# Two of four units of the recurrence's output product, moved behind the last head's output in the program

## The chip, the core and the metric

One core of one Trainium2 chip runs the whole program once. The metric is the device time of one execution in microseconds (us), here the median of three runs of the kernel before. Five engines work beside each other, each through its own queue of instructions and strictly in that queue's order: TensorE (PE in the profile, with its weight loads as PEld), VectorE (DVE), ScalarE (ACT), GpSimd (POOL), and SyncE (SP), which issues the loads from HBM. They wait for each other by semaphores.

## What is computed

Two model blocks follow each other on a sequence of 512 tokens of width 1024. The change touches the first half of the second block only. There a normed input is projected to two mixers: a matrix memory (four heads of width 128, run forward and backward, with the context's 256 tokens in front) and a gated recurrence (four heads of width 128). Both outputs are normed, gated and projected back into the residual stream. Cut to that:

```python
pl = _modulate(_rmsnorm(xl, norm1_w[l]), sh1, sc1) @ w_in[l]
pc = _modulate(_rmsnorm(xc, norm1_w[l]), sh1c, sc1c) @ w_in[l]
ml_l, ml_c = _mlstm_mixer(pl[..., :ML_COLS], pc[..., :ML_COLS], ...)   # norm(h) * sigmoid(o)
hg_l, hg_c = _hgrn_mixer(pl[..., ML_COLS:], pc[..., ML_COLS:], ...)    # norm(o) * silu(g)
xl = xl + g1 * (jnp.concatenate([ml_l, hg_l], axis=-1) @ w_out[l])
```

The rows of `w_out` that belong to the recurrence need only `hg_l`, which is ready before the matrix memory starts. So this part of the product (`wout2h` in the kernel) may be done anywhere in the matrix memory's stretch.

## The kernel before, in words

Everything is kept with the model's width on the 128 partitions and the 512 tokens along the free dimension. Every fp32 product is made of three passes over operands split in a high and a low part: `mm3` records matmuls at L211, L212 and L213, each 128x512. A weight unit of 128x1024 comes by `wload`: a load of 512 KB (tile `raw`, two buffers, L225), a copy of the high part on ScalarE (`wh`, three buffers, L189) and the low part on VectorE or GpSimd (`wl`, three buffers, L192). `wload` runs at a raised priority, so that it stands some places ahead of where it was called.

The program is written head by head, and a scheduler then sets each engine's queue: it follows the written order as priority, but takes an instruction earlier or later where its own timing model says that the operands come so. Tiles of one tag rotate over a fixed number of buffers: 4 PSUM banks for `mm`, 3 for `aux`, 1 for `sm`. A tile that comes round to a bank waits until the former tile in it has been read.

`mlstm` (L1773) runs the matrix memory. Per head `h`:
- `pj(h)` projects keys and queries and convolves them (`caccm`, nine taps: on VectorE mostly, a few by ScalarE as `ctapm` and GpSimd), and `silu` makes `mk` and `mq` of them on ScalarE. This runs one head ahead.
- `ml_weights` (L1919) makes the decay weights `mW`, one per direction: a row broadcast by a matmul (L1916, tile `ps_sm`, tag `sm`), an add on VectorE, four exponentials on ScalarE. For heads 2 and 3 it is called at the end of heads 0 and 1.
- `ml_within` (L1931) transposes the keys (L1939, `mkT`), makes the scores (L1944), and multiplies them into `mW` on VectorE.
- `ml_states` (L1950) makes the chunk states of each direction: five matmuls (L1970, `ps_aux`), chained decays on VectorE and ScalarE (`mC`), and a row broadcast (L1916) that scales the queries (`mqw`).
- `ml_out` (L1986) makes the outputs, four groups of four matmuls (L1994, L1995); each group takes one of the three `aux` banks, and VectorE and ScalarE read it out (`mdn`, `myt`, `yml`).

In the last turn of the loop, where no next head is to be projected, two other pieces stand ahead of the last head's states: `hgout((0, 1, 2))`, three of the four units of the recurrence's output product (24 matmuls per unit: two output tiles of four `mm3`, reading `mhH` and `mhL`; each tile is added to the residual `x` by VectorE in `res`), and `proj_tok` of `w2o`, the gate's projection (four weight units, 96 matmuls, which read `wh` with `h3H`). `proj_tok` accumulates all four units into four `mm` tiles at once and hands them over in `pso`. Behind the loop their sigmoids follow on ScalarE (`og`), then the fourth unit, `hgout((3,))`. The calls of `bact` between two `batch()` calls are ordered on ScalarE as a group, so that its function tables are swapped seldom: the four `og` stand behind the silu of head 3, which stands behind the exponentials of head 3's weights. After that come the head norms (transposes at L1617, `moH`, `moL`) and the matrix memory's part of the output product (`wout2m`).

Quoted, since the order matters:

```python
            for h in range(4):
                self.ahead = 400
                if h < 3:
                    nxt = silu(*pj(h + 1))
                else:
                    pso = []
                    hgout((0, 1, 2))
                    self.proj_tok(I["w2o"], lambda b, ps: pso.append(ps), False)
                self.ahead = 150
                Cq = self.ml_states(pw, h, kT, kq[1])
```

Of the kernel before, what the change touches and what calls it, by code (L numbers as in the profile page):

```python
# [179 lines left out]
class Kern:  # L180
# [1592 lines left out]
    def mlstm(self, st, hs, cs):  # L1773
# [25 lines left out]
        def pj(h):  # L1799
            pl, pc = self.proj2(I["w2k"][h], hs, cs)  # L1800
            raw = p.tile([128, T], F32, name="mraw", tag="mraw", bufs=2)
            self.act(raw, pl)
            rc = p.tile([128, TC], F32, name="mrawc", tag="mrawc", bufs=1)
            self.act(rc, pc)
            k = self.conv(raw, self.cwm[:, 4 + h], p, 8, 64, 3, "m")
            kc = self.conv(rc, self.cwm[:, 4 + h], p, 1, 256, 0, "mc")
            pl, _ = self.proj2(I["w2q"][h], hs, None)
            raw = p.tile([128, T], F32, name="mraw", tag="mraw", bufs=2)
            self.act(raw, pl)
            q = self.conv(raw, self.cwm[:, h], p, 8, 64, 3, "m")  # L1810
            return k, kc, q

        def silu(k, kc, q):
            kf = p.tile([128, NT], F32, name="mk", tag="mk", bufs=2)
            self.bact(kf[:, 0:TC], kc, AF.Silu)
            self.bact(kf[:, TC:], k, AF.Silu)
            qf = p.tile([128, T], F32, name="mq", tag="mq", bufs=2)
            self.bact(qf, q, AF.Silu)
            return kf, qf
# [9 lines left out]
        def res(m, ps, sl):  # L1829
            self.stt(self.x[m][:, sl], ps, g1[:, m:m + 1], self.x[m][:, sl], mul, add)  # L1830

        def hgout(us):

            for u in us:
                W = self.wload(I["wout2h"][u])
                for i in range(2):
                    ps = self.mmtile()
                    for k in range(4):
                        c = slice(512 * i + 128 * k, 512 * i + 128 * k + 128)
                        self.mm3(ps, (W[0][:, c], W[1][:, c]), (self.mHL[0][:, k], self.mHL[1][:, k]), k == 0, k == 3)  # L1840
                    res(2 * u + i, ps, slice(0, T))

        with ExitStack() as st1:
            pw = self.pool(st1, "mlw")
            self.batch()
            W = [self.ml_weights(pw, i) for i in range(2)]
            self.batch()
            kq = silu(*kq)
            kT = self.ml_within(pw, 0, *kq, W[0])
# [3 lines that stand above are left out]
                    nxt = silu(*pj(h + 1))  # L1853
                else:
                    pso = []
                    hgout((0, 1, 2))
                    self.proj_tok(I["w2o"], lambda b, ps: pso.append(ps), False)
                self.ahead = 150
                Cq = self.ml_states(pw, h, kT, kq[1])
                if h < 3:  # L1860
                    kq = nxt
                    kT = self.ml_within(pw, h + 1, *kq, W[h + 1])
                self.ml_out(pw, h, W[h], *Cq, yml)
                if h < 2:
                    self.batch()
                    W.append(self.ml_weights(pw, h + 2, "sm"))
                    self.batch()
            self.batch()
            for b in range(4):
                o = p.tile([128, 512], F32, name="og", tag=("mraw", "caccm")[b % 2], bufs=2)  # L1870
                self.bact(o, pso[b], AF.Sigmoid)
                self.tt(o, o, self.mlw, mul, nc.gpsimd)
                og.append(o)
            hgout((3,))

            self.stc.close()
            pm = self.pool(st, "mlm", side="right")
            mo = [pm.tile([128, 4, T], F32R, name="mo" + n) for n in "HL"]
            for h in range(4):
                self.head_norm(p, yml, h, og, mo)  # L1880
            self.dump("yml", yml)
# [240 lines left out]
```

## Time and profile before

| what | us |
|---|---|
| median of 3 runs (1603.66 to 1607.11) | 1603.7 |
| the profiled execution, its own time | 1606.45 |
| its span, first to last instruction | 1604.7 |
| TensorE busy in the span | 1551.7 (97%) |
| VectorE busy | 1107.8 (69%) |
| ScalarE busy | 764.3 (48%) |
| GpSimd busy | 385.0 (24%) |

The span is what the trace shows; the execution's own time has 1.75 us more around it. Busy time of TensorE counts matmuls whose ends are modelled and overlap, so its waits are better read from the starts of its matmuls, in order of time. In the rows that stand further down, a line of the timeline has the start, the time taken, engine, source line, operation, output and inputs, and in brackets how long the engine sat idle before it and what released it.

### The profile page before, as it was taken

The page shows a single profiled execution, that of the slowest core. Times are in us where ns is not written, and L with a number is a line of the kernel's source. Part 1 is how long each engine was busy: PE and PEld are TensorE (multiplying, and loading weights), DVE is VectorE, ACT ScalarE, POOL GpSimd, SP SyncE. Part 2 cuts the span into 40 slices and gives each one's busy share as a digit, 9 for nine tenths or more (in the row PEclk, how much of TensorE's full clock was granted, in tenths as well). Part 3 has the DMA queues.
Part 4 walks back from the last instruction along what each step waited for, and adds up shares of the span by engine and source line. Part 5 has one row for each costly group of instructions (what it writes and reads, how often), then busy time and mean ns, then how long its engine had stood idle before and what let it go on. Part 6 is the DMA issues. An engine that isn't in the chain of part 4 may idle for free.

```text
span 1604.7 us, 22771 instructions
## 1 busy us (share of the span) xinstructions
PE 1551.7 (97%) x8577; PEld 1296.0 (81%) x8577; DVE 1107.8 (69%) x2055; ACT 764.3 (48%) x1405; POOL 385.0 (24%) x327
## 2 busy tenths in 40 slices
PE   7999997999999999999999999999989999999997
PEld 6778786677888888888888888878879888888886
DVE  8887546676679754863436777478877798676745
ACT  5453536563444213452346777646654664343322
POOL 1110124113000000000020001314320897556552
PEclk9999999999999999999999999999999999999998
DMA  5222411004356764833222111111211322232322
GB/s 192 82 74 67 133 56 47 14 21 133 103 199 214 245 197 130 258 111 103 82 65 71 33 51 54 47 56 64 66 59 66 102 95 92 98 100 92 96 86 82
DMA packets 58733, 157.84 MB, mean 98 GB/s; under 512 B 11904, under 2 KB 18816, under 8 KB 58496
## 3 DMA queue, kind: packets, MB, share of 16 engines
q1 hardware_dynamic: 58624, 156.40, 30.4%
q8 instruction: 67, 1.10, 0.3%
q14 instruction: 42, 0.34, 0.1%
HBM read 152.57 MB, written 2.10 MB: 96 GB/s over the span
## 4 chain that ended last, share of the span: by engine, by line
PE 81%; DVE 11%; ACT 5%; issue 2%; POOL 1%; DMA 1%; SPq 0%; DVEq 0%; ACTq 0%
PE ps_mm L211 23%; PE ps_mm L213 22%; PE ps_mm L212 22%; PE ps_sm L1129 2%; DVE wl L192 2%; DVE caccm L201 2%; PE ps_mm L1118 1%; PE ps_aux L1574 1%; ACT L189 1%; ACT wh L189 1%; PE ps_sm L787 1%; DVE caccf L201 1%; PE ps_aux L1563 1%; PE ps_aux L1096 1%; PE ps_sm L1590 0%
## 5 line engine op out<-in xcount | busy, mean ns | idle before, releaser
L189 ACT ACTIVATE wh<-raw 128x1024 fp32r<-128x1024 f32 (+3 forms) x234 | 236.8, 1013 | 498.7 <-PE ps_mm L212 361.6
L192 DVE TENSOR_TENSOR wl<-raw,wh 128x1024 fp32r<-128x1024 f32 (+2 forms) x162 | 196.7, 1215 | 99.3 <-ACT wh L189 93.5
L201 DVE SCALAR_TENSOR_TENSOR caccf<-ps_mm,cwf,caccf 128x441 f32<-128x441 f32 (+2 forms) x278 | 188.5, 695 | 30.9 <-ACT ctapf L189 24.8
L192 POOL TENSOR_TENSOR wl<-raw,wh 128x1024 fp32r<-128x1024 f32 (+2 forms) x72 | 160.7, 2233 | 158.7 <-ACT wh L189 158.6
L213 PE MATMUL ps_mm<-h4H,wl 128*128 128x512 f32 (+1 forms) x352 | 131.2, 375 | 0.0
L212 PE MATMUL ps_mm<-h4L,wh 128*128 128x512 f32 (+1 forms) x352 | 131.1, 375 | 0.0
L211 PE MATMUL ps_mm<-h4H,wh 128*128 128x512 f32 (+1 forms) x352 | 129.7, 377 | 0.6 <-DVE caccf L201 0.4
L192 POOL TENSOR_TENSOR rr<-rv,nhalf 128x2 f32<-128x2 f32 x9 | 8.5, 946 | 431.3 <-DVE rv L198 431.3
L211 PE MATMUL ps_mm<-h2H,wh 128*128 128x512 f32 (+1 forms) x280 | 103.8, 372 | 0.0
L213 PE MATMUL ps_mm<-h2H,wl 128*128 128x512 f32 (+1 forms) x280 | 103.6, 371 | 0.0
L212 PE MATMUL ps_mm<-h2L,wh 128*128 128x512 f32 (+1 forms) x280 | 103.6, 371 | 0.0
L211 PE MATMUL ps_mm<-aH,wh 128*128 128x512 f32 (+1 forms) x272 | 102.6, 377 | 0.5 <-DVE x L192 0.5
L213 PE MATMUL ps_mm<-aH,wl 128*128 128x512 f32 (+1 forms) x272 | 102.7, 378 | 0.0
L212 PE MATMUL ps_mm<-aL,wh 128*128 128x512 f32 (+1 forms) x272 | 102.4, 377 | 0.0
L1265 DVE CUSTOM_DVE_ANT_0 msc<-wmod,cB,cols 128x1024 bf16<-128x1024 f32 x64 | 82.0, 1282 | 21.1 <-DMA wmod<-in_wmod 20.7
L211 PE MATMUL ps_mm<-hH,wh 128*128 128x512 f32 x216 | 85.2, 402 | 8.2 <-ACT hH L189 8.2
L213 PE MATMUL ps_mm<-hH,wl 128*128 128x512 f32 x216 | 85.4, 396 | 1.5 <-DVE wl L192 1.5
L212 PE MATMUL ps_mm<-hL,wh 128*128 128x512 f32 x216 | 85.4, 396 | 0.0
L213 PEld LDWEIGHTS ps_mm<-h4H,wl 128*128 128x128 f32 x352 | 66.2, 188 | 12.3
L212 PEld LDWEIGHTS ps_mm<-h4L,wh 128*128 128x128 f32 x352 | 66.2, 188 | 12.3 <-DVE h4L L201 0.4
L211 PEld LDWEIGHTS ps_mm<-h4H,wh 128*128 128x128 f32 x352 | 65.0, 188 | 13.4 <-issue 0.8
L211 PE MATMUL ps_mm<-faH,wh 128*128 128x512 f32 (+1 forms) x194 | 72.3, 373 | 0.0
(548 smaller groups left out, 4039.2 us busy)
## 6 DMA issues: line engine op xcount, KB each, us to landing
raw<-in_wup SPq DMA_DIRECT2D x76, 512.0 KB, 3.5
wmod<-in_wmod SPq DMA_DIRECT2D x48, 512.0 KB, 4.3
raw<-in_wdn SPq DMA_DIRECT2D x32, 512.0 KB, 3.5
raw<-in_win SPq DMA_DIRECT2D x28, 512.0 KB, 3.3
raw<-in_wout SPq DMA_DIRECT2D x8, 512.0 KB, 3.5
raw<-in_wdn2a SPq DMA_DIRECT2D x8, 512.0 KB, 3.5
raw<-in_wdn2b SPq DMA_DIRECT2D x8, 512.0 KB, 3.4
raw<-in_wdn2c SPq DMA_DIRECT2D x8, 384.0 KB, 3.2
```

The costliest lines, as they stand in the source:

```text
L189: return self.nc.scalar.activation(o, i, f, **k)
L192: return (e or self.nc.vector).tensor_tensor(o, a, b, op)
L201: return self.nc.vector.scalar_tensor_tensor(o, a, s, b, op0, op1)
L211: mm(ps, wh, xh, start=start, stop=False)
L212: mm(ps, wh, xl, start=False, stop=False)
L213: ins = mm(ps, wl, xh, start=False, stop=stop)
L787: nc.tensor.matmul(py[32 * pl:32 * pl + 32, 128 * st:128 * st + 128], w[:, q4.start + pl, st], x[:, pl, 0:128], start=i == 0, stop=i == 2, ...
L1096: nc.tensor.matmul(S[:, :n2], self.qs[:, 2 * j + g, c], self.ks[:, 2 * br + g, :n2], start=True, stop=False)
L1118: nc.tensor.transpose(tp[:, 128 * b:128 * b + 128], P[g, i][:, 128 * b:128 * b + 128], self.ident)
L1129: nc.tensor.matmul(O[64 * g:64 * g + 64, 128 * i:128 * i + 128], self.V[:, b, c:c + 64], PT[g][:, 128 * b:128 * b + 128], start=br == 0 an ...
L1265: ins = nc.vector.tensor_tensor_reduce(sc, w, cB[:, c], 1.0, bm[:, m:m + 1], OP.mult, OP.add, acc)
L1563: nc.tensor.matmul(ps[k0:k0 + m, j, c:c + m], e[:, k0:k0 + m], e[:, q0:q0 + m], start=True, stop=True, tile_position=(0, k0), skip_group_c ...
```

## The change

The call in the last turn keeps unit 0 alone, and units 1 and 2 are called after the loop, behind `ml_out` of the last head and ahead of the sigmoids.

```diff
@@ -1853,7 +1853,7 @@
                     nxt = silu(*pj(h + 1))
                 else:
                     pso = []
-                    hgout((0, 1, 2))
+                    hgout((0,))
                     self.proj_tok(I["w2o"], lambda b, ps: pso.append(ps), False)
                 self.ahead = 150
                 Cq = self.ml_states(pw, h, kT, kq[1])
@@ -1865,6 +1865,7 @@
                     self.batch()
                     W.append(self.ml_weights(pw, h + 2, "sm"))
                     self.batch()
+            hgout((1, 2))
             self.batch()
             for b in range(4):
                 o = p.tile([128, 512], F32, name="og", tag=("mraw", "caccm")[b % 2], bufs=2)
```

The instructions are the same in number and shape; the scheduler orders them anew. Below L1867 every line number is one higher in the changed kernel.

First place: TensorE's queue at the states of head 1, right behind head 0's output and the recurrence's unit 0. Before:

```order
L1970 MATMUL ps_aux<-mvs,mkT 128x130 x3
L213 MATMUL ps_mm<-mhH,wl 128x512
L211 MATMUL ps_mm<-mhH,wh 128x512
L1970 MATMUL ps_aux<-mvs,mkT 128x130 x2
L212 MATMUL ps_mm<-mhL,wh 128x512
L213 MATMUL ps_mm<-mhH,wl 128x512
```

Now:

```order
L1971 MATMUL ps_aux<-mvs,mkT 128x130 x3
L213 MATMUL ps_mm<-mhH,wl 128x512
L211 MATMUL ps_mm<-wh,h3H 128x512
L1971 MATMUL ps_aux<-mvs,mkT 128x130 x2
L212 MATMUL ps_mm<-wl,h3H 128x512
L213 MATMUL ps_mm<-wh,h3L 128x512
```

The 48 matmuls of units 1 and 2 (`mhH`) are gone from here, and the gate's projection (`h3H`) starts in their place.

Second place: TensorE's queue at the states of head 2 and the second weight row of head 3. Before, a part of the gate's projection stands between them:

```order
L1916 MATMUL ps_sm<-nM,sel_9157 128x512
L211 MATMUL ps_mm<-wh,h3H 128x512
L212 MATMUL ps_mm<-wl,h3H 128x512
L213 MATMUL ps_mm<-wh,h3L 128x512
L1916 MATMUL ps_aux<-wi,sel_9157 128x512
L211 MATMUL ps_mm<-wh,h3H 128x512
L212 MATMUL ps_mm<-wl,h3H 128x512
L213 MATMUL ps_mm<-wh,h3L 128x512
L1970 MATMUL ps_aux<-mvs,mkT 128x130 x5
L211 MATMUL ps_mm<-wh,h3H 128x512
```

Now:

```order
L1971 MATMUL ps_aux<-mvs,mkT 128x130 x5
L213 MATMUL ps_mm<-wh,h3L 128x512
L211 MATMUL ps_mm<-wh,h3H 128x512
L212 MATMUL ps_mm<-wl,h3H 128x512
L213 MATMUL ps_mm<-wh,h3L 128x512
L1917 MATMUL ps_sm<-nM,sel_9157 128x512
L1917 MATMUL ps_aux<-wi,sel_9157 128x512
L1971 MATMUL ps_aux<-mvs,mkT 128x130 x5
L1917 MATMUL ps_aux<-wi,sel_9157 128x512
L1940 MATMUL ps_aux<-ident,mk 128x128 x6
L211 MATMUL ps_mm<-mhH,wh 128x512
```

The projection has ended by then: the small steps of head 2 and the transposes of head 3's keys stand in a row, and the next large matmul is the first of unit 1. Units 1, 2 and 3 follow it, all ahead of the last head's output matmuls in this queue.

Third place: ScalarE's queue around the four sigmoids `og`. Before:

```order
L189 ACTIVATE mW<-mW,mgaT 128x128 x4
L189 ACT_TABLE_LOAD
L189 ACTIVATE mk<-caccmc 128x256
L189 ACTIVATE mk<-caccm 128x512
L189 ACTIVATE mq<-caccm 128x512
L189 ACT_TABLE_LOAD
L189 ACTIVATE og<-ps_mm 128x512
L189 ACTIVATE mC<-ps_aux,mgdec 128x130
L189 ACTIVATE og<-ps_mm 128x512 x2
```

Now:

```order
L189 ACTIVATE mW<-mW,mgaT 128x128 x4
L189 ACT_TABLE_LOAD
L189 ACTIVATE mk<-caccmc 128x256
L189 ACTIVATE mk<-caccm 128x512
L189 ACTIVATE mq<-caccm 128x512
L189 ACT_TABLE_LOAD
L189 ACTIVATE og<-ps_mm 128x512 x4
L189 ACTIVATE mkT<-ps_aux 128x384 x2
```

The sigmoids keep their place behind head 3's exponentials, two table loads and the silu. On SyncE's queue the loads change from three units of `wout2h`, four of `w2o`, one of `wout2h` to one, four, three.

## Rows read from the trace of the kernel before

**Rows 1.** Page, part 1 (busy time by engine) and part 4 (chain that ended last).

```profile
PE 1551.7 (97%) x8577; PEld 1296.0 (81%) x8577; DVE 1107.8 (69%) x2055; ACT 764.3 (48%) x1405; POOL 385.0 (24%) x327
...
PE 81%; DVE 11%; ACT 5%; issue 2%; POOL 1%; DMA 1%; SPq 0%; DVEq 0%; ACTq 0%
```

**Rows 2.** Busy time in two stretches: us, PE, PEld, DVE, ACT, POOL, clock, DMA.

```profile
1160.00:1170.00 10.00, 10.00 (x60) 8.73 (x59) 6.79 (x15) 8.26 (x18) 3.16 (x4) 1.00 0.25 95
...
1190.00:1200.00 10.00, 7.69 (x59) 6.69 (x59) 7.08 (x28) 4.48 (x14) 0.20 (x1) 1.00 0.01 2
```

**Rows 3.** Timeline of PE: head 1's states, gate projection's ends, fourth unit's ends.

```profile
1128.10 0.83 PE L1970 MATMUL ps_aux<-mvs,mkT 128*128 128x130 f32 x6
...
1142.50 0.39 PE L211 MATMUL ps_mm<-wh,h3H 128*128 128x512 f32 x1
...
1173.62 0.39 PE L213 MATMUL ps_mm<-wh,h3L 128*128 128x512 f32 x1
1173.85 0.40 PE L211 MATMUL ps_mm<-mhH,wh 128*128 128x512 f32 x1
...
1182.76 0.47 PE L213 MATMUL ps_mm<-mhH,wl 128*128 128x512 f32 x1
```

**Rows 4.** Timeline of PE: waits of the output groups and states, first head-norm transposes.

```profile
1152.52 0.39 PE L213 MATMUL ps_mm<-wh,h3L 128*128 128x512 f32 x1
1153.89 0.46 PE L1994 MATMUL ps_aux<-mlv,mW 128*128 128x130 f32 x2 [0.99 <-DVE mW L201]
...
1187.01 1.35 PE L1970 MATMUL ps_aux<-mvs,mkT 128*128 128x130 f32 x10 [0.65 <-DVE mdn L192]
...
1192.26 0.49 PE L1994 MATMUL ps_aux<-mlv,mW 128*128 128x130 f32 x2 [1.35 <-DVE mqw L201]
...
1195.92 0.49 PE L1994 MATMUL ps_aux<-mlv,mW 128*128 128x130 f32 x2 [0.71 <-DVE yml L201]
...
1196.92 1.04 PE L1617 MATMUL ps_aux<-ident,yml 128*128 128x128 f32 x8
```

**Rows 5.** Timeline of DVE: convolution taps, score multiplies, the weights' add of head 3.

```profile
1145.51 1.54 DVE L201 SCALAR_TENSOR_TENSOR caccm<-mraw,cwm,caccm 128x441 f32<-128x441 f32 x1 [0.62 <-POOL caccm L192]
1146.97 2.17 DVE L192 TENSOR_TENSOR wl<-raw,wh 128x1024 fp32r<-128x1024 f32 x1
1149.06 3.49 DVE L201 SCALAR_TENSOR_TENSOR caccm<-mraw,cwm,caccm 128x441 f32<-128x441 f32 x4
1152.47 1.28 DVE L201 SCALAR_TENSOR_TENSOR mW<-ps_aux,mW 128x512 f32<-128x512 f32 x2
...
1161.69 1.23 DVE L192 TENSOR_TENSOR wl<-raw,wh 128x1024 fp32r<-128x1024 f32 x1 [1.42 <-ACT wh L189]
1162.83 0.68 DVE L192 TENSOR_TENSOR mW<-ps_sm,mneg 128x512 f32<-128x512 f32 x1
```

**Rows 6.** Timeline of ACT: table load after head 3's exponentials, first sigmoid.

```profile
1168.92 1.28 ACT L189 ACT_TABLE_LOAD   x1
...
1172.98 0.60 ACT L189 ACTIVATE og<-ps_mm 128x512 f32<-128x512 f32 x1
```

**Rows 7.** Timeline of POOL in that stretch, and the loads of the projection.

```profile
1143.11 7.01 POOL L192 TENSOR_TENSOR caccm<-caccm,ctapm 128x448 f32<-128x448 f32 x5
...
raw<-in_w2o SPq DMA_DIRECT2D x4, 512.0 KB, 3.5
```

**Rows 8.** Clock in two stretches (columns as in rows 2), and PE's timeline at the fall.

```profile
1052.00:1056.00 4.00, 4.00 (x12) 3.12 (x11) 3.91 (x6) 2.34 (x2) 0.00 (x0) 0.57 0.00 0
...
1188.00:1192.00 4.00, 2.57 (x16) 1.74 (x14) 3.86 (x13) 1.09 (x4) 1.01 (x1) 1.00 0.02 4
...
1050.93 0.56 PE L1760 MATMUL ps_sm<-ident,mgt 64*128 64x64 f32 x6 [1.48 <-DVE mgbe L1717]
...
1052.40 0.63 PE L212 MATMUL ps_mm<-wl,h3H 128*128 128x512 f32 x1
1052.83 0.63 PE L213 MATMUL ps_mm<-wh,h3L 128*128 128x512 f32 x1
```

## The prediction, made before the changed kernel was run

> **What bounds the kernel now.** I read the page first, then the windows, then TensorE's timeline, since the change moves work on that engine alone. The page gives TensorE 97% of the span and 81% of the chain that ended last [rows 1]. So what counts is TensorE's waits, and the question is whether the change makes more or fewer of them. The windows say where they are: from 1160 to 1170 it is busy for 10.00 of 10 us, from 1190 to 1200 for 7.69 [rows 2]. The first stretch holds the gate's projection, the second the end of the last head with nothing to put between its steps. The change takes large matmuls out of the first and puts them nearer the second.
>
> The stretch that the change reorders starts at 1128.10 with head 1's states [rows 3] and ends at 1196.92 with the head norms' transposes [rows 4], so it takes 68.8 us. The instructions in it are the same in both kernels, so only waits can differ. Counted in TensorE's order there are 169 large matmuls, 0.23 apart (1173.62 to 1173.85 [rows 3]; 0.2275 over long runs), 48 output matmuls and 30 state matmuls at about 0.22 (the trace shows two records for each of these), 9 row broadcasts at 0.23, and 20 transposes and scores with 2.6 together: 38.4 + 10.7 + 6.6 + 2.1 + 2.6 = 60.4, which leaves 8.3 or so of waits. **Where they are:** behind the last large matmul (1182.76 + 0.23) TensorE comes to the last head's output at 1192.26, 9.3 us for 16 output matmuls, 10 state matmuls and 2 broadcasts, which is 4.5 of work: 4.8 of waits, for VectorE's `mdn`, `yml` and `mqw`. The third output group of head 1 waits 1.1 for `mW` (1152.52 + 0.23 to 1153.89), the last group of head 3 waits 0.9 for `yml` [rows 4], and 1.5 is spread thin.
>
> **The change, part by part.** Nothing is added or removed. Units 1 and 2 stood behind 1128.10 and up to 1142.50 [rows 3]; now the projection stands there, and three things follow.
>
> *First, the output of head 1.* In the changed order 74 large matmuls stand ahead of its third group, not 79, so TensorE is there 1.1 us earlier, at 1151.6, or at 1151.2 if the thin waits ahead of it fall away. The group needs an `aux` bank, which VectorE frees by the multiplies into `mW`. These end at 1152.47 + 1.28 = 1153.75 now [rows 5], and VectorE's order puts one more tap ahead of them (0.87 at this stretch's rate, 3.49 for four), so between 1153.75 and 1154.6. I take their end at 1154.1, so the wait is 2.5 to 2.9 in place of 1.1. I take 2.9.
>
> *Second, the hole.* This is the large term. With 97 large matmuls, 15 state matmuls, 16 output matmuls and 14 small ones ahead of it (22.1 + 3.3 + 3.6 + 2.2 = 31.2, and the 2.9 waited), the projection ends at about 1162.2, where before it ended at 1173.85 [rows 3]. It holds all four `mm` banks until ScalarE's sigmoids read them, and unit 1 needs one. The sigmoids have not moved in ScalarE's order: they stand behind head 3's exponentials, a table load that ran at 1168.92, the silu, and a second load, so the first started at 1172.98 [rows 6] and freed its bank at 1173.58. Before, the bank was wanted at 1173.85, so nobody waited. What can come earlier is the start of that chain, VectorE's add into `mW` at 1162.83. A split of 1.23 stood ahead of it with 1.42 idle before that [rows 5]; in the new order this split stands behind it. So the add goes between 1160.3 (idle and split gone) and 1161.6 (split gone); I take 1160.7, nearer the early end, as the idle is put down to the split's operand alone. From the add to the end of the first sigmoid it was 1173.58 - 1162.83 = 10.75, and ScalarE's steps between them stay in a nearly closed row, so unit 1 starts at about 1171.5 (bounds 1171.0 to 1172.4). Between 1162.2 and 1171.5 TensorE has 2.3 us of small work (5 state matmuls, 3 broadcasts, 6 transposes): a wait of 7.0.
>
> *Third, the end.* From unit 1 on there are 72 large matmuls, 10 state matmuls, 2 broadcasts, 4 scores and 32 output matmuls to go: 16.4 + 2.2 + 0.5 + 0.8 + 7.1 = 27.0. Units 1, 2 and 3 stand between the last states in TensorE's queue, so the 4.8 of waits there are covered, less 0.9 that I leave because `mqw` comes late from VectorE behind a split. The last group's 0.9 for `yml` [rows 4] stays, as no unit stands behind the last head's output. So the stretch ends at 1171.5 + 27.0 + 1.8 = 1200.3, not 1196.92: **+3.4** (as waits: 2.9 + 7.0 + 1.8 = 11.7 against 8.3, the same).
>
> *What I cost at nothing.* Loads: the same eight units of 512 KB in another order, each landing 3.5 us after its issue [rows 7], with two buffers to run ahead in. I cost them at nothing. The cover is the 5.5 us that one unit's 24 matmuls take; without it a unit would start up to 3.5 late. GpSimd's queue swaps one state scaling with a tap, also nothing, since TensorE has other work there.
>
> *The clock.* After 1.48 us idle at 1050.93 TensorE's granted clock fell to the lower of its two levels, 1.2 GHz: the window from 1052 to 1056 has 0.57 and large matmuls stand 0.43 apart (1052.40 to 1052.83). Yet from 1188 to 1192, with gaps up to 1.35 [rows 4] and only 2.57 of 4 busy, it stayed 1.00 [rows 8]. The hole is longer than either and nearly empty, so I take one fall as at 1052: 4 x (1 - 0.57) = 1.7. Bounds: 0 and 3.4 (twice that).
>
> The Trainium skill ("TensorE: Matmul & The Clock Gate", Part 1) says that TensorE runs at its lower clock after idling and gets the full clock back only after a stretch of continuous work. The fall at 1052 agrees, the window at 1188 doesn't show how much idling it takes; by that rule the sum has the 1.7, by the window at 1188 it hasn't.
>
> **Sum.** +3.4 + 1.7 = +5.1. The profiled execution took 1606.45 with a span of 1604.7; the median of the runs is 1603.7, 2.75 below that execution. I add the sum to the median: **1608.8**, and a span of 1609.8 where a profile shows it. About 0.3% (4.8 us) is what a measurement of this kernel can tell from no change.
>
> **Rivals.** *The clock holds.* For it: 1.00 in the window at 1188 [rows 8]. Against: a gap of some 7 us is far longer than any there. Then +3.4: 1607.1. *A second fall or a longer one.* The wait at 1151 to 1154 is longer than the idle that ended at 1050.93, and the small steps of the hole are spread over it. Then 3.4 for the clock: 1610.5, and with the sigmoids at their late bound 1611.5. *The other side: the sigmoids come early and the end's cover is worth more than the hole.* Mechanism: VectorE's stretch before 1155 is stretched by GpSimd; a tap of `caccm` took 1.54 and a split 2.17 there, against 0.87 a tap and 1.23 a split later [rows 5], while GpSimd ran five `caccm` steps for 7.01 [rows 7]. If the new order sets these apart, VectorE gains up to 0.7 + 0.9 = 1.6, the add comes by as much earlier and the wait at 1154 shrinks. The point from which it decides: each us that the first sigmoid comes earlier is a us less, so with 3.4 us earlier, its end by 1168.1 and no clock fall, the change is even; with the hole gone entirely it gains 3.6 (7.0 - 3.4): 1600.1. Against: ScalarE's two table loads (1.28 for the one in [rows 6]), silu and exponentials stand in that chain whatever VectorE does, and the new order has the same amount of GpSimd work in that stretch. So 1600.1 to 1603.7, and I put it at 1602.5. *The change doesn't do what it says*, in part, whatever case holds: units 1 and 2 are written behind the last head's output but stand ahead of it in TensorE's queue. So they cover its states and not its output groups; had they stood behind, the 0.9 of the last group would be gone as well, 0.9 less in every case.
>
> The Trainium skill ("GPSIMD Engine Reference", section 8) says that GpSimd and VectorE share SBUF interfaces, so that they slow each other. The 1.54 and 2.17 agree; by that rule the order of the two engines, not only their amount of work, sets when the add comes.
>
> **How the numbers follow.** Forecast 0.45 (own range 1607.5 to 1610.3), clock holds 0.27, second or longer fall 0.13, other side 0.15. The range leaves out the end of the other side below 1602 and the worst of the longer fall: 1602.0 to 1612.5. The bound of 0.3% is 1608.5, so the forecast splits: two thirds of it and all of the longer fall count as slower, with a fifth of the case of the held clock (late sigmoids), 0.30 + 0.13 + 0.06 = 0.49; faster by over 4.8 would need 1598.9, below even the hole's complete loss, which also needs waits of now to go: 0.05 of the other side; the rest is within, 0.46.
>
> **What would show it.** Right: the projection ends near 1162, then TensorE's first matmul on `mhH` starts near 1171.5 and is released by ScalarE's `og`; a granted clock well below 1 in the windows behind it; a wait of about 2.9 before head 1's third output group, released by VectorE's `mW`; no gap over 1 us between the last states. Wrong: unit 1's start below 1168 or above 1173, waits left between the last states with units at hand, or large matmuls waiting for `wh` or `wl` (loads late) anywhere in the stretch.

## The result and the profile after

| what | before | after |
|---|---|---|
| median of four runs, us | 1603.95 | 1612.88 (1611.97 to 1614.09) |
| ratio, 95% interval | | 1.0051 (1.0035 to 1.0067) |
| the profiled execution, own time | 1606.45 | 1611.97 |
| its span | 1604.7 | 1610.3 |

The change makes the kernel slower by 0.35% to 0.67%, 5.6 to 10.7 us, where +5.1 was forecast. A fourth run has moved the median of before from 1603.7 to 1603.95. A second set of runs of the change, further down, has one execution of 3111.14 us among its five, which the ratio leaves out; it is the one that was profiled, so no trace of that set is read. The two profiled executions lie 5.6 apart by their spans and the medians 8.9. That gap has two ends: the profile of before is 2.5 above its median, that of after 0.9 below. So the medians are read for the size, and the profiles for the cause, inside the stretch of [rows 3, 4], from head 1's states to the head norms' first transposes. Ahead of it nothing has changed: in the thirteen profiles that are read here TensorE has the same 6241 matmul records there with the same tiles in the same order. Yet the stretch begins anywhere from 1124.95 us (e12) to 1130.52 (e1), while behind it 407.3 to 407.9 us follow in each. So its length, 75.6 us against 68.8, is the cleanest measure of the change: +6.8.

Parts 1 and 4 of the page of the changed kernel, against [rows 1]:

```profile
PE 1549.4 (96%) x8577; PEld 1293.6 (80%) x8577; DVE 1109.4 (69%) x2055; ACT 763.3 (47%) x1405; POOL 384.0 (24%) x327
...
PE 81%; DVE 10%; ACT 5%; issue 2%; DMA 1%; POOL 1%; SPq 0%; DVEq 0%; ACTq 0%
```

The same number of instructions, and TensorE is busy for 2.3 us less in a span that is 5.6 longer: it stands idle for longer. TensorE's timeline of the changed kernel shows the waits (L1971, L1917, L1940, L1995 are [rows 3, 4]'s lines, one higher):

```profile
1126.89 0.83 PE L1971 MATMUL ps_aux<-mvs,mkT 128*128 128x130 f32 x6
...
1153.22 0.46 PE L1995 MATMUL ps_aux<-mlv,mW 128*128 128x130 f32 x2 [2.61 <-DVE mW L201]
...
1161.26 0.40 PE L213 MATMUL ps_mm<-wh,h3L 128*128 128x512 f32 x1
1161.49 0.40 PE L1917 MATMUL ps_sm<-nM,sel 128*128 128x512 f32 x1
...
1168.02 1.64 PE L1940 MATMUL ps_aux<-ident,mk 128*128 128x128 f32 x6 [1.04 <-DVE mC L201]
1170.97 0.80 PE L211 MATMUL ps_mm<-mhH,wh 128*128 128x512 f32 x1 [1.31 <-ACT og L189]
1171.56 0.63 PE L212 MATMUL ps_mm<-mhL,wh 128*128 128x512 f32 x1
1171.99 0.63 PE L213 MATMUL ps_mm<-mhH,wl 128*128 128x512 f32 x1
...
1175.65 0.39 PE L213 MATMUL ps_mm<-mhH,wl 128*128 128x512 f32 x1
1175.88 0.40 PE L211 MATMUL ps_mm<-mhH,wh 128*128 128x512 f32 x1
...
1201.49 0.49 PE L1995 MATMUL ps_aux<-mlv,mW 128*128 128x130 f32 x2 [0.71 <-DVE yml L201]
...
1202.49 1.04 PE L1617 MATMUL ps_aux<-ident,yml 128*128 128x128 f32 x8
```

The wait of 2.61 for `mW` stands where [rows 4] has 0.99. The projection's last matmul starts at 1161.26, and unit 1's first at 1170.97, released by the sigmoid: 9.5 us between 1161.49 and 1170.97, with only small work in it. Unit 1 begins at 0.43 a matmul and is at 0.23 again from 1175.65. The states of the last head have units between them now. ScalarE and VectorE of the changed kernel, against [rows 6] and [rows 5]:

```profile
1159.82 1.28 ACT L189 ACT_TABLE_LOAD   x1
...
1164.97 1.26 ACT L189 ACTIVATE mW<-mW,mgaT 128x128 f32<-128x128 f32 x4
1166.25 1.28 ACT L189 ACT_TABLE_LOAD   x1
...
1169.02 1.28 ACT L189 ACT_TABLE_LOAD   x1
1170.32 2.06 ACT L189 ACTIVATE og<-ps_mm 128x512 f32<-128x512 f32 x4
```

```profile
1144.35 4.50 DVE L201 SCALAR_TENSOR_TENSOR caccm<-mraw,cwm,caccm 128x441 f32<-128x441 f32 x3 [0.44 <-POOL caccm L192]
...
1149.90 1.97 DVE L201 SCALAR_TENSOR_TENSOR caccm<-mraw,cwm,caccm 128x504 f32<-128x504 f32 x3
1151.80 1.27 DVE L201 SCALAR_TENSOR_TENSOR mW<-ps_aux,mW 128x512 f32<-128x512 f32 x2
...
1159.30 0.68 DVE L192 TENSOR_TENSOR mW<-ps_sm,mneg 128x512 f32<-128x512 f32 x1
```

The four sigmoids stand in a row behind two table loads, and from 1164.97 to the first of them ScalarE has no gap. The add that opens their chain starts at 1159.30; in the changed kernel everything is 1.2 us earlier from the start of the stretch on (1126.89, not 1128.10), so that is 1160.5 on the clock of before. The windows of the changed kernel (columns as in [rows 2]):

```profile
1150.00:1160.00 10.00, 7.39 (x43) 6.21 (x42) 9.01 (x24) 3.11 (x11) 0.00 (x0) 1.00 0.25 72
1160.00:1170.00 10.00, 6.59 (x30) 4.41 (x28) 6.13 (x17) 9.49 (x20) 3.87 (x5) 0.76 0.26 88
1170.00:1180.00 10.00, 9.03 (x41) 7.63 (x42) 7.09 (x11) 3.14 (x7) 5.11 (x4) 0.73 0.00 0
1190.00:1200.00 10.00, 9.42 (x57) 8.08 (x56) 7.92 (x19) 1.75 (x3) 0.00 (x0) 1.00 0.17 54
```

TensorE's 10.00 of [rows 2] in the second window has become 6.59, and its 7.69 in the last has become 9.42. The change did what it says: the waits at the end are filled. They were filled at the price of a hole, and of a clock that was at its lower level in it and behind it.

### The profile page after: what moved, and what is told of

Same layout as the page of the kernel before. It is cut to its first block, busy times and chain, and to the rows that moved or that the text cites. A ratio compares the mean times of both kernels' runs of the same rounds, so it can differ in the third digit from the quotient of the medians.

```text
span 1610.3 us, 22769 instructions
## 1 busy us (share of the span) xinstructions
PE 1549.4 (96%) x8577; PEld 1293.6 (80%) x8577; DVE 1109.4 (69%) x2055; ACT 763.3 (47%) x1405; POOL 384.0 (24%) x327
## 4 chain that ended last, share of the span: by engine, by line
PE 81%; DVE 10%; ACT 5%; issue 2%; DMA 1%; POOL 1%; SPq 0%; DVEq 0%; ACTq 0%
PE ps_mm L211 23%; PE ps_mm L212 22%; PE ps_mm L213 22%; DVE caccm L201 2%; PE ps_sm L1129 2%; DVE wl L192 2%; PE ps_mm L1118 1%; PE ps_aux L1574 1%; ACT L189 1%; ACT wh L189 1%; DVE caccf L201 1%; PE ps_aux L1563 1%; PE ps_sm L787 1%; PE ps_aux L1096 1%; PE ps_sm L1590 0%
## 5 line engine op out<-in xcount | busy, mean ns | idle before, releaser
L211 PE MATMUL ps_mm<-hH,wh 128*128 128x512 f32 x216 | 84.7, 399 | 10.1 <-ACT hH L189 10.1
L213 PEld LDWEIGHTS ps_mm<-h4H,wl 128*128 128x128 f32 x352 | 66.2, 188 | 12.3
L212 PEld LDWEIGHTS ps_mm<-h4L,wh 128*128 128x128 f32 x352 | 66.2, 188 | 12.3 <-DVE h4L L201 0.4
```

Of the source, the lines that this page charges most:

```text
L211: mm(ps, wh, xh, start=start, stop=False)
L212: mm(ps, wh, xl, start=False, stop=False)
L213: ins = mm(ps, wl, xh, start=False, stop=stop)
```

## The experiments

The change has the four runs of the result; each other row has five or more, and the time of before beside it is that of the same chip. From each profile I take one more account, in the stretch from head 1's first state matmul to the first transpose of the head norms: its length, what the clock took (in windows of 1 us, TensorE's busy time times one minus the granted clock, added up), and what is left as waits once the 60.5 us of work are subtracted (68.8 less 8.3; 66.0 in the kernel with fillers). The last two columns are a way of booking and not two separate costs: work slowed inside a hole whose end another engine sets is booked as slow clock, though it lengthens nothing. In the change that holds for 1.6 of the 3.8.

| kernel | median, us | before | ratio (95%) | stretch | slow clock | waits |
|---|---|---|---|---|---|---|
| before | 1603.95 | | | 68.8 | 0.0 | 8.3 |
| the change | 1612.88 | 1603.95 | 1.0051 (1.0035 to 1.0067) | 75.6 | 3.8 | 11.3 |
| the change again | 1613.13 | 1606.19 | 1.0047 (1.0033 to 1.0060) | not read | | |
| e1 banks freed | 1609.67 | 1605.36 | 1.0030 (1.0017 to 1.0042) | 73.0 | 1.6 | 10.9 |
| e2 one unit moved | 1611.79 | 1605.36 | 1.0040 (1.0027 to 1.0052) | 74.0 | 3.4 | 10.1 |
| e3 fillers | 1610.39 | 1605.36 | 1.0036 (1.0022 to 1.0049) | 75.1 | 1.7 | 7.4 |
| e5 one unit, one held | 1611.05 | 1605.36 | 1.0032 (1.0019 to 1.0044) | 74.9 | 3.4 | 11.0 |
| e8 multiplies first | 1614.22 | 1606.19 | 1.0055 (1.0042 to 1.0069) | 74.8 | 2.1 | 12.2 |
| e12 freed, held | 1615.21 | 1606.19 | 1.0059 (1.0047 to 1.0072) | 78.0 | 3.7 | 13.8 |
| e11 freed, held, multiplies first | 1611.40 | 1606.19 | 1.0040 (1.0027 to 1.0052) | 73.5 | 1.7 | 11.3 |
| e13 groups later | 1612.90 | 1605.19 | 1.0047 (1.0035 to 1.0060) | 76.0 | 3.1 | 12.3 |
| e14 freed, groups later | 1610.96 | 1605.19 | 1.0037 (1.0025 to 1.0050) | 74.7 | 1.7 | 12.5 |
| e16 as e14, half a unit held | 1615.30 | 1605.19 | 1.0061 (1.0049 to 1.0074) | 79.1 | 4.6 | 14.0 |
| e17 before, half a unit held | 1610.55 | 1605.19 | 1.0025 (1.0014 to 1.0037) | 73.9 | 3.3 | 10.1 |

The stretch follows the medians: what it has over 68.8 is within 2.2 us of the difference of the medians in each row. None of the kernels is faster than before.

**The change again.**

> The changed kernel itself, on the chip and beside the kernels that follow. Theory H: 6 to 9 us over the kernel before; the wait of 2.6 us ahead of head 1's third output group and the hole of some 9 us behind the projection are there again. Where the slow clock falls (behind the first wait, in the hole, or both) may differ from profile to profile by 1.7 us.

+6.9 us beside another set of runs of before, within the 6 to 9 expected, and an interval that overlaps the first. Only its times are used.

**e1, the banks freed.** VectorE copies each projection tile to SBUF when it is complete.

```diff
-                    self.proj_tok(I["w2o"], lambda b, ps: pso.append(ps), False)
+                    self.proj_tok(I["w2o"], lambda b, ps: pso.append(self.copied(p, b, ps)), False)
...
-                o = p.tile([128, 512], F32, name="og", tag=("mraw", "caccm")[b % 2], bufs=2)
-                self.bact(o, pso[b], AF.Sigmoid)
+                o = pso[b]
+                self.bact(o, o, AF.Sigmoid)
...
+    def copied(self, p, b, ps):
+        t = p.tile([128, 512], F32, name="og", tag=("mraw", "ogc")[b % 2], bufs=2)
+        self.ts(t, ps, 0.0, OP.add)
+        return t
```

> The changed kernel, but VectorE copies each of the four projection tiles out of its mm bank as soon as it is complete (four 128x512 reads more), and the sigmoids then work in SBUF. Theory H (the hole: unit 1 waits for the banks until the sigmoids, and the clock falls meanwhile): the first mhH matmul follows the projection's end within 1.5 us, the granted clock stays 1.00 between 1160 and 1180, and of the change's cost the 7.0 us of the hole and some 2 us of slow clock go. But nothing keeps units back now, so they are used up before the last head's states and the 4.8 us of waits there come back: 1605 to 1608. Rival L (the cost is the new order of loads, or the longer wait at head 1's output): the time stays at 1611 or more and the gap is only moved.

TensorE's timeline of e1, then VectorE's:

```profile
1156.83 0.67 PE L2000 MATMUL ps_aux<-mlv,mW 128*128 128x130 f32 x2 [2.60 <-DVE mW L201]
...
1166.50 0.40 PE L213 MATMUL ps_mm<-wh,h3L 128*128 128x512 f32 x1
1166.74 0.39 PE L211 MATMUL ps_mm<-mhH,wh 128*128 128x512 f32 x1
...
1184.27 0.55 PE L1945 MATMUL ps_aux<-ident,mk 128*128 128x128 f32 x3 [1.58 <-DVE mqw L201]
```

```profile
1171.38 0.68 DVE L201 SCALAR_TENSOR_TENSOR mqw<-ps_aux,mq 128x512 f32<-128x512 f32 x1
1176.83 2.00 DVE L201 SCALAR_TENSOR_TENSOR yml<-yml,fr,og 128x128 f32<-128x128 f32 x2 [4.77 <-POOL og L192]
...
1183.54 0.68 DVE L201 SCALAR_TENSOR_TENSOR mqw<-ps_aux,mq 128x512 f32<-128x512 f32 x1
```

The hole is gone: unit 1 starts one matmul behind the projection. That settles its cause: the four banks, held until the sigmoids. But the stretch fell by 2.6 us only, and the median, 1609.67, lies between the two forecasts, 1605 to 1608 and 1611 or more. The waits went from 11.3 to 10.9: they came up elsewhere. The second fence shows where some of them come from: VectorE's queue now has head 0's norm (`yml` with `og`) ahead of head 2's second `mqw`, and idles 4.77 us for the sigmoid and GpSimd's product behind it. TensorE then waits 1.58 for that `mqw`. The sigmoids' time is waited for by two ways, the banks and VectorE's queue, and the copies opened only one. The last head's states, which no unit covers now, wait 1.46 for `mdn`, as was expected. And 1.6 us of slow clock stand behind the wait for `mW`, where the profile of the change has none.

Two things limit this reading. The copies are work too: four of 0.68 us on VectorE, and the first sigmoid starts 44.3 us after the stretch does, not 43.4 as in the change. No run here says how much of e1's remaining loss is theirs. And e1's six times lie in two groups, 1606.98 to 1608.19 and 1611.15 to 1612.99, of which the profile shows the slowest; its stretch begins 2.4 us later than that of before.

**e2 and e5, one unit moved.** The call in the loop is `hgout((0, 1))`, the one behind it `hgout((2,))`; in e5 unit 3's matmuls are also ordered behind the last head's first state matmul:

```diff
-        mm(ps, wh, xh, start=start, stop=False)
+        i0 = mm(ps, wh, xh, start=start, stop=False)
+        if self.hold is not None:
+            self.tc.add_manual_dep(i0.ins, self.hold, NOSYNC, reason="order")
+            self.hold = None
...
-            hgout((3,))
+            hgout((3,), self.st1)
```

> Only unit 2 moves behind the loop, units 0 and 1 stay ahead of the projection. Theory H: the projection ends 5.5 us later than in the changed kernel, near 1167, against sigmoids that still come near 1171 to 1173; 1 to 2 us of small work lie between, so a wait of 2 to 4 us, no or a short fall of the clock, and no cover left for the last states: 1604 to 1608, clearly under half of the cost of the full change. Rival N (each unit moved costs the same, from cover lost where it stood): half of the change's cost, 1608.5.

> As with unit 2 alone moved, and unit 3 also held back in TensorE's order until the first state matmul of the last head. Theory H: the wait for the banks is 2 to 4 us as there, unit 3's 24 matmuls cover the 4.8 us of waits between the last states, but head 2's outputs and head 3's transposes have only unit 2: 1601 to 1605, below the kernel with unit 2 alone moved. Rival K (total cover is what counts, wherever it stands): the same time as with unit 2 alone moved, within 1 us.

TensorE's timeline of e2, and two of its windows:

```profile
1153.53 0.46 PE L1995 MATMUL ps_aux<-mlv,mW 128*128 128x130 f32 x2 [2.47 <-DVE mW L201]
...
1174.14 0.50 PE L211 MATMUL ps_mm<-mhH,wh 128*128 128x512 f32 x1 [2.36 <-ACT og L189]
```

```profile
1150.00:1160.00 10.00, 7.53 (x35) 6.09 (x34) 9.75 (x24) 2.37 (x8) 0.00 (x0) 0.83 0.14 52
...
1170.00:1180.00 10.00, 7.64 (x32) 6.07 (x31) 5.90 (x7) 6.72 (x11) 5.84 (x5) 0.83 0.01 3
```

The wait for the banks is in the range given, 2.36 us. Yet one unit moved costs 6.4 us, where the change costs 6.9 to 8.9: the wait for `mW` stands there in full (2.47), and each of the two waits was followed by a clock of 0.83 over 10 us, 1.7 a time. Both theories missed it; the cost does not go by units. In e5 no wait is left among the last states, but head 3's scores wait 0.47 and head 2's outputs 1.19: its stretch is 0.9 longer than e2's, its median 0.7 lower. That is rival K: 1601 to 1605 was expected of the other theory, and it is 1611.05.

**e3, fillers in the hole.**

```diff
+            fill = self.mmtile(tag="sm")
+            for i in range(24):
+                nc.tensor.matmul(fill, self.mHL[0][:, i % 4, 0:128], self.mHL[0][:, 0], start=i == 0, stop=i == 23)
             hgout((1, 2))
```

> The changed kernel with 24 matmuls 128x512 added (5.5 us of TensorE work, result unused, into the sm bank) that its order places in the hole, between the states of head 2 and the transposes of head 3. Theory H with the clock as a cost of its own: the granted clock in the hole and behind it is 0.95 to 1.00 instead of 0.5, unit 1's first ten matmuls take 2.3 us instead of 4.4, and in spite of the added work the time falls by 1 to 3 us, to 1610 to 1612. Rival C (the slow clock lies beside waits and costs nothing): the time stays or rises, 1613 to 1618.

TensorE's timeline of e3, and its windows:

```profile
1161.72 0.40 PE L213 MATMUL ps_mm<-wh,h3L 128*128 128x512 f32 x1
...
1163.63 5.06 PE L1870 MATMUL ps_sm<-mhH 128*128 128x512 f32 x21
...
1170.15 0.48 PE L211 MATMUL ps_mm<-mhH,wh 128*128 128x512 f32 x1
...
1170.70 0.39 PE L213 MATMUL ps_mm<-mhH,wl 128*128 128x512 f32 x1
1170.93 0.40 PE L211 MATMUL ps_mm<-mhH,wh 128*128 128x512 f32 x1
```

```profile
1160.00:1170.00 10.00, 9.86 (x53) 8.01 (x52) 4.57 (x11) 9.49 (x21) 2.61 (x4) 1.00 0.16 55
1170.00:1180.00 10.00, 9.77 (x59) 8.30 (x58) 8.77 (x18) 2.21 (x6) 6.54 (x6) 1.00 0.00 1
```

With 5.5 us of added matmuls the stretch is 0.5 us shorter than the change's. The hole has its length from the sigmoids, so work in it is free. The clock stays at 1.00 and unit 1's matmuls stand 0.23 apart from the start, not 0.43, which saves 2.2 us on them. Of these 0.9 came back as time: from unit 1's start to the end of the stretch it is 30.65 us, against 31.52 in the change, partly because three of head 3's transposes stand behind that start here. The slow clock that is left, 1.7, follows the wait for `mW` there (2.59 us). The median of 1610.39 is in the range given. By times alone, though, the fillers and the change cannot be told apart, since their intervals overlap; the granted clock tells them apart.

**e8 and e13, the first wait.** In e8 two of the six taps ahead of VectorE's multiplies are ordered behind them; in e13 TensorE comes to head 1's third and fourth output groups later. Their core:

```diff
+                if self.tapdep is not None and i == 5:
+                    self.tc.add_manual_dep(ins.ins, self.tapdep, NOSYNC, reason="order")
```

```diff
+                if h == 3:
+                    self.tc.add_manual_dep(self.g3.ins, self.pn[27], NOSYNC, reason="order")
+                    self.tc.add_manual_dep(self.g4.ins, self.pn[30], NOSYNC, reason="order")
```

> The changed kernel, but VectorE does head 2's multiplies into mW ahead of two taps that stood before them, and TensorE's order follows. Theory H: the wait ahead of head 1's third output group falls from 2.6 to 1.0 to 1.5 us and the projection ends as much earlier, but unit 1 still waits for the sigmoids, so the hole gets as much longer: within 1.5 us of the changed kernel. Rival V (VectorE's lateness there is a cost of its own, added to the hole's): 2 to 4 us below the changed kernel.

> The changed kernel with head 1's third and fourth output groups moved back in TensorE's order by 11 and more projection matmuls, so that VectorE's multiplies into mW are done when it gets there. Theory H (waits in series, the hole ends when the sigmoids come): the wait of 2.6 us goes, the projection ends some 2.5 us earlier, and the hole is longer by nearly as much, since the sigmoids do not come earlier: within 1.5 us of the changed kernel. Rival V (the wait is a cost of its own beside the hole): 2.5 to 4 us below the changed kernel, 3 to 5 over before.

TensorE's timeline of e13:

```profile
1166.41 0.76 PE L1923 MATMUL ps_aux<-wi,sel 128*128 128x512 f32 x1 [2.91 <-DVE yml L201]
...
1173.01 0.73 PE L211 MATMUL ps_mm<-mhH,wh 128*128 128x512 f32 x1 [2.71 <-ACT og L189]
```

In e13 the wait for `mW` is gone altogether, and in e8 it fell from 2.61 to 1.94 (1.0 to 1.5 was expected). Neither is faster than the change: +7.7 (e13) and +8.0 us (e8) against before, where the change had +6.9 and +8.9. From the first state matmul (1129.69 in e13) to unit 1 it is 43.3 us, against 44.1 in the change (1170.97 - 1126.89). So the two waits stand in series ahead of one event, and the hole takes up 1.8 of the 2.6 that the first gives back. In e8 the sigmoids themselves come earlier, and unit 1 with them, 42.3 us after the start; but behind unit 1 the stretch has 32.5 us and not 31.5, so 1.0 of the 1.8 gained is lost again. Theory H holds here, rival V falls.

**e12, e11, e14, e16, e17: placing the cover by hand.** e12 and e11 are e1 with unit 2 ordered behind head 3's first transpose and unit 3 behind the last head's first state matmul, e11 with e8's edit too. e14 is e1 with e13's edit, e16 adds a hold on unit 3's second tile, and e17 is the kernel before with that hold and the third group six matmuls later.

> Banks freed by copies as in the first experiment, and unit 2 held back in TensorE's order until the transposes of head 3's keys, unit 3 until the last head's first state matmul. Theory H: no hole, and now also cover for the last states: against the kernel with freed banks alone (4.2 us over before in the stretch) some 3 us less, so within 2 us of the kernel before; what is left is the wait at head 1's third output group, 1.5 us more than before, with a slow clock of 1.7 us behind it. Rival K (only the total of waits counts, cover moved is cover lost): the same as with freed banks alone, 4 to 5 us over before.

> As the one before, and the multiplies into mW ahead of two taps. Theory H: without a hole behind it the wait at head 1's third output group is a cost of its own, so taking 1 to 1.5 us off it, and with it the slow clock of 1.7 us behind it, shows fully here, unlike with the hole: 2 to 3 us below the kernel without it, 1 to 4 us under the kernel before. Rival V2 (the taps set the end of the chain to the exponentials, and come later now): no gain, as the kernel without it.

> Banks freed by copies as in the first experiment, and head 1's third and fourth output groups moved back as in the one before. Theory H: without the hole the wait of 2.6 us and the slow clock behind it (1.7) are the cost that was left over before in that experiment (4.2 us in the stretch), so 2.5 to 4 us less than with freed banks alone and within 2 us of the kernel before. Rival P (what was left there is the four copies on VectorE or the lost cover of the last states): no gain over freed banks alone, 4 us over before.

> As the one before, and unit 3's second tile (12 matmuls, 2.7 us) held back in TensorE's order until the last head's first state matmul. Theory H: it covers 2 to 3 us of waits between the last states but leaves head 2's outputs bare, where waits of 1 to 2 us come up: 0 to 2 us below the one without it. Rival K (cover moved is cover lost): the same or slower.

> The kernel before, with head 1's third output group moved back by 6 projection matmuls and unit 3's second tile held back as in the one before: no unit is moved behind the loop. Theory H: the 1.1 us of wait ahead of the third group go, and of the 4.8 us of waits among the last head's steps 2 to 3 are covered against 1 to 2 new ones in head 2's outputs: 1 to 3 us below the kernel before. Rival K: the same as before within 1 us, or slower.

e12 is the slowest but one, 9.0 us over before, where one theory had it within 2 and the other 4 to 5 over. Its VectorE timeline, and its TensorE timeline at the same place:

```profile
1165.79 0.68 DVE L201 SCALAR_TENSOR_TENSOR mqw<-ps_aux,mq 128x512 f32<-128x512 f32 x1
1171.20 1.96 DVE L201 SCALAR_TENSOR_TENSOR yml<-yml,fr,og 128x128 f32<-128x128 f32 x2 [4.73 <-POOL og L192]
...
1173.94 0.67 DVE L201 SCALAR_TENSOR_TENSOR mqw<-ps_aux,mq 128x512 f32<-128x512 f32 x1
```

```profile
1168.25 0.39 PE L1927 MATMUL ps_aux<-wi,sel 128*128 128x512 f32 x1
1174.77 0.88 PE L1950 MATMUL ps_aux<-ident,mk 128*128 128x128 f32 x3 [6.12 <-DVE mqw L201]
```

VectorE idles 4.73 us for `og` with head 2's `mqw` behind it in its queue. TensorE's transposes need the `aux` bank that this `mqw` reads, and unit 2 was held back behind those transposes: 6.12 us idle. The hold turned a hidden wait into a bare one. e11, whose order differs on both engines, has 1.86 at that place and 4.5 us less in the stretch. It is still 5.2 over before, and 1 to 4 under was expected. The 4.5 is more than e8's edit was expected to give, and since it moved the whole order, not the first wait alone (1.93 there against 2.60), I don't put the gain down to that wait.

e14 refutes what I expected of it, that the wait for `mW` and the slow clock behind it were what was left in e1; rival P, the copies or the lost cover, had no gain, and there is none. The wait for `mW` is gone from it and the stretch grew by 1.6, with new waits of 2.32 (`mqw`) and 1.24 (`yml`) later on. e16 and e17 show rival K: with half a unit held for the last states, e16 grows by 4.4 over e14, and e17 by 5.1 over before. TensorE's timeline of e17:

```profile
1182.93 0.46 PE L2005 MATMUL ps_aux<-mlv,mW 128*128 128x130 f32 x2 [2.12 <-DVE mdn L2013]
```

```profile
1180.00:1190.00 10.00, 7.79 (x41) 6.91 (x40) 6.26 (x25) 3.19 (x13) 0.78 (x1) 0.83 0.15 52
1190.00:1200.00 10.00, 7.38 (x42) 6.34 (x40) 7.01 (x23) 2.05 (x4) 0.23 (x1) 0.83 0.15 54
```

Its waits rose by 1.8 only, but one of them, 2.12 in head 2's outputs, is longer than any in the stretch before (1.35), and the clock was at 0.83 in the two windows from 1180 to 1200: 3.3 of the 5.1 by the table's booking.

## Why the prediction was right, and where its sum was not

**The waits: right in kind and place, 1.2 us short in sum.** By the starts of its matmuls the wait at head 1's third group was put at 2.9 and is 2.76 (1150.23 + 0.23 to 1153.22; 2.61 of it idle). The projection's end was put at 1162.2 and unit 1's start at 1171.5; on the clock of before they are 1162.7 and 1172.2, so the hole was put at 9.3 us and is 9.5. The add into `mW` was put at 1160.7 and is 1160.5. The sigmoid's chain behind it took 11.6 (1159.30 to about 1170.9), not 10.75. What lengthened it is the table load ahead of the exponentials. In the kernel before it ended with the add (1162.83 + 0.68); in the changed kernel, at 1159.82 + 1.28, it ends 1.1 us behind it. ScalarE before:

```profile
1162.27 1.28 ACT L189 ACT_TABLE_LOAD   x1
```

The cover of the last head came as said: the states that had 4.8 us of waits among them have matmuls now. That units 1 to 3 would not cover its output groups held too: the last group still waits 0.71 for `yml`, as in [rows 4]. Behind unit 1 the stretch has 31.5 us; less 27.0 of work and the 2.2 that its slowed matmuls cost, that leaves 2.3 of waits, put at 1.8.

**The loads: right.** No large matmul waits for `wh` or `wl` in the stretch.

**The clock: the mechanism right, the term a little small.** I took one fall of the length seen at 1052, 1.7 us, and gave a longer one 0.13. In the changed kernel's window from 1165 to 1175 the granted clock is 0.51, and the table has 3.8 us of TensorE's work lost. But 1.6 of that was lost on the small matmuls in the hole, and the hole ends with the sigmoids, ahead of which ScalarE has no gap from 1164.97 on: by my sum this costs nothing. Behind the hole 2.2 were lost, on unit 1's first ten matmuls. That is the term, and it lies between my 1.7 and the 3.4 of the second rival (whose 1611.5 with late sigmoids should read 1611.4: 1610.5 and 0.9).

So in the stretch the sum was 1.7 short, 5.1 against 6.8, in three terms that were all too small: unit 1's start by 0.7, the waits behind it by 0.5, the clock by 0.5. Counted as waits, the first two make 4.6 in place of 3.4 (75.6 less 60.5 of work, 2.2 of clock and the 8.3 that were there before). The fillers show the mechanism of the last: filled, the same hole has 1.00.

```profile
1165.00:1175.00 10.00, 7.33 (x21) 5.33 (x22) 6.19 (x11) 8.09 (x16) 5.43 (x6) 0.51 0.17 55
```

The Trainium skill ("TensorE: Matmul & The Clock Gate", Part 1) says that an idle TensorE falls to its lower clock and gets the full one back after continuous work; this window and the fillers agree with it.

**The base: off by what other falls do.** The medians differ by 8.9 in the first comparison and 6.9 in the second, the stretch by 6.8. Ahead of it the clock falls at places that vary: before has 0.57 from 1052 to 1056 [rows 8] and 0.91 from 1040 to 1060, after has 1.00 over those 20 us. So one profile's distance to the median, 2.5 and -0.9, is of the size of the effect, and the sum against a single profile could not be better than about 2 us.

**The range: reached at its end.** It ended at 1612.5. The median is 1612.88; 1603.7 times the ratio is 1611.9. Both lie above the 1607.5 to 1610.3 of the forecast case. The forecast gave a loss clear of noise a chance of 0.49, so it leaned towards what came only a little; the places and releasers of the waits, which came as written, speak more for it than the size does.

**The rival on the other side: refuted where it can be seen.** I put the price of the hole at all of its 7 us, so that without it the change would gain 3.6. e1 took the hole away and kept a loss of 0.17% to 0.42%. The step that fails is "with the hole gone entirely it gains 3.6": it let the other waits stand as they were. They did not: VectorE's queue waits for the same sigmoids (4.77 us in e1), and the waits of the heads' small steps come up where the large matmuls aren't (e5, e12, e16, e17). What I did not try is to move the head norm behind head 2's `mqw` on VectorE, or the sigmoids ahead of the silu; whether e1 would gain with either stays open.

**GpSimd beside VectorE: seen, and not decisive.** Three taps took 1.50 each while GpSimd ran its five steps (until 1148.4) and 0.66 each from 1149.90 on. In [rows 5, 7] a tap and a split stood beside GpSimd, now three taps do, so the new order did not set the two engines apart. The Trainium skill ("GPSIMD Engine Reference", section 8) says that the two share SBUF interfaces; the taps agree.

## What to carry to other kernels

A block of work that covers waits is worth what it covers there less what it bares where it stood, and a PSUM bank that a late reader holds puts that reader's whole chain ahead of whatever needs the bank next: find the event that the block will wait for before moving it. Price a new wait on TensorE in two terms, the idle itself and the work done at the lower clock behind it; here the second was 2.2 us on 4.6 of added waits. Work slowed inside a hole is not part of it where another engine ends the hole. In the stretch of the kernel before, with no wait above 1.35, the clock stayed at 1.00; that gathering short waits into a long one can lose by the clock alone was not tested by itself. And one that takes a wait away should look for the next queue that stands behind the same event, here VectorE's.

## What was not expected of the hardware

The clock does not answer every wait alike. In the change TensorE stood idle for 2.61 us ahead of 1153.22 and the window from 1150 to 1160 has 1.00; in e1 it stood for 2.60 at the same instruction, and the matmuls behind it are 0.43 a pair where the same pairs take 0.22 in the kernel before (1154.19 to 1154.41); TensorE's timeline of e1:

```profile
1157.30 0.64 PE L2001 MATMUL ps_aux<-mC,mqw 128*128 128x130 f32 x2
1157.73 0.64 PE L2000 MATMUL ps_aux<-mlv,mW 128*128 128x130 f32 x2
```

The same happened in e2 (2.47), e3 (2.59), e5 (2.44) and e12 (2.60), each with 0.83 over that window. Where the wait there was shorter, 1.94 in e8 and 1.93 in e11, the window has 1.00; yet the idle of 1.48 ahead of 1050.93 was followed by a fall [rows 8]. So one profile shows which falls an execution had, not which it always has, and a term of the clock is better forecast as a range with a profile of the same wait at either end.
